# One branch a step, and another order of fetches, in a two-layer hybrid decoder trunk

## The chip, the core and the metric

The kernel runs as one program on one core of a Trainium2 chip. The metric is device time in microseconds, the median of several executions. The core has a matrix engine (TensorE, PE in the profile), VectorE (DVE), ScalarE (ACT), GpSimd (POOL) and SyncE (SP). Each takes its instructions in order. In this kernel SP issues nearly all DMAs, from memory into SBUF, and a DMA that must wait for its buffer holds up every DMA behind it.

## What is computed

256 tokens of width 1024 go through two layers, all in float32:

```python
h = x
for i in range(2):
    mix = forgetting_attention(h, ...) if i == 0 else ssd_mixer(h, ...)
    h = layer_norm(ALPHA * h + mix, ln_mix_g[i], ln_mix_b[i])
    ffn = swiglu(h, ...) if i == 0 else moe_swiglu(h, ...)
    h = layer_norm(ALPHA * h + ffn, ln_ffn_g[i], ln_ffn_b[i])
    h = h + (p[i] @ ple_w_proj[i]) * sigmoid(h @ ple_w_gate[i])
```

The second layer's feed-forward part has 8 experts, of which each token takes 2. An expert has a gate and an up matrix of 1024 x 3584 and a down matrix of 3584 x 1024:

```python
for e in range(8):
    y_e = (silu(x @ w_gate[e]) * (x @ w_up[e])) @ w_down[e]
    out = out + gates[..., e:e+1] * y_e
```

## The kernel before

All weights lie in memory as chunks of 128 x 2048 floats, 1024 KB each, in the order of their use. In SBUF there are 22 slots of one chunk each, `sf[0]` to `sf[21]` (`sr[i]` is the same memory under the type fp32r). Slots 20 and 21 are called TH and TL: up to the end of the mixer they hold the transposed tokens, split into a high and a low rounded part, and after it they take chunks like the others. Slots 0 and 1 hold token buffers in the expert stage, so 20 slots are left for chunks there. The constants `ck` (identity, triangles, iota) are a tile of their own.

**Layers up to the mixer** take each float32 product as three fp32r products (`mm3`, L213 to L215) of parts split by ScalarE (L153) and VectorE (L156). `fetch` issues a chunk's DMA on SP in four pieces (L139) into a slot of the ring `rq`; `load` adds the two splits, with a slot of the ring `wq` for the high part.

**The state-space mixer** works on 8 groups g. Its steps are written out by hand: `channels` (projections), `conv`, `mix_a` to `mix_y` (the scan inside a group), `decay(q)` (factors for two groups, `decs`), and `w_out(g, t)` (the output projection). Ahead of the experts, slots that are done with are refilled by `next_chunk(n)` (its DMA is at L1012), which fetches the next chunk of a fixed list `order` into slot n. These calls stand by hand among the mixer's steps: slots 13 and 14 in the group loop at g == 4, right behind `decay(3)`, which is the last to read them; slot 15, then TH and TL, then eleven more in the tail of the mixer, and the last four behind it.

**The experts** run as 56 steps (e, f), 7 per expert; a step takes 512 of the 3584 columns and has six chunks, four for gate and up and two for down. A step gathers no tokens itself: once per expert up to 96 tokens are gathered by a matmul with a one-hot matrix (`gather`). The first 64 of them go through `gate_up0` (L1386) and `down0` (L1422) with 64 columns of the array, the other 32 through `gate_up1` (L1393) and `down1` (L1429). The latter two stand each in an If on TensorE alone, `over(e)`, taken when expert e has more than 64 tokens; `L1591` and `L1580` are their lines. `turn_u` transposes the step's activations (L1412, L1413). The order of a step i on TensorE is: gate_up0(i), If gate_up1(i), down0(i-1), If down1(i-1), turn_u(i). Each `next_chunk` of a slot stands behind the part that reads it last. `y_out` copies the expert's sums out of PSUM (L1435, L1437) and `scatter` adds them to the tokens in the next step, with one float32 matmul per token half and column half (L1442).

In expert 7, f == 0, `pr`, the operand pT of the last projection (256 KB), is fetched (L1619) behind that step's `next_chunk` calls; it is multiplied at L1628 in f == 2 and 3. At f == 4 `beyond` (L1483) is an If on all engines around a long loop for experts with more than 96 tokens; with this data it is jumped over. Behind the experts come the last scatter, the LayerNorm and the gated embedding.

From the mixer on, the order on PE, ACT, DVE and SP is the order of the text (`manual_schedule`).

Of the kernel before, what the change touches and what calls it, by code (L numbers as in the profile page):

```python
# [17 lines left out]
P = 128  # L18
D = 1024
# [34 lines left out]
def trunk_kernel(ctx, tc, ws, xtok, xT, pT, lnp, cst, wsm, cw, gn, vec, out):  # L54
# [4 lines left out]
    nc.alloc_sbuf_tensor("slots", [P, N_SLOT * 2048 + 16], FT)  # L59
    base = (nc.sbuf_base - (N_SLOT * 2048 + 16) * 4 + 63) // 64 * 64  # L60
# [4 lines left out]
    sf = [place(f"sf{i}", 2048, FT, i) for i in range(N_SLOT)]  # L65
    sr = [place(f"sr{i}", 2048, FR, i) for i in range(N_SLOT)]
# [167 lines left out]
    ck = const.tile([P, K_END], FT, name="ck")  # L234
# [598 lines left out]
    with tc.tile_pool(name="ssd", bufs=1, reuse_waits="tile") as sd, tc.tile_pool(name="ssd2", bufs=2, reuse_waits="tile") as s2p:  # L833
        cwt = sd.tile([P, 32, 5], FT, name="cwt")
# [425 lines left out]
        next_chunk(TH)  # L1260
        next_chunk(TL)
# [13 lines left out]
        for n in rq[:-1] + wq[:-1] + [12, 16, 17]:  # L1275
            next_chunk(n)
# [25 lines left out]
    with tc.tile_pool(name="moe", bufs=1, reuse_waits="tile") as mo:  # L1302
        res = tokens(1)
        hx = sf[18].rearrange("p (t k q) -> p t k q", t=T, k=KT)
        strb = mo.tile([P, P], BF, name="strb")
        oneb = mo.tile([P, P], BF, name="oneb")
# [65 lines left out]
        def turn_s(s, name="sT", bufs=2):  # L1372
# [3 lines left out]
            sT = mo.tile([SLOTS, T, P], FT, name=name, bufs=bufs)  # L1376
            nc.vector.tensor_copy(sT, ps[0:SLOTS, 0:S].rearrange("p (t q) -> p t q", t=T))
            return sT
# [30 lines left out]
        def turn_u(u0, u1):  # L1409
# [3 lines left out]
            nc.tensor.transpose(ps[:, 2 * P:3 * P], u1, ident)  # L1413
            uT = mo.tile([P, 3 * P], FT, name="uT")
            nc.vector.tensor_copy(uT, ps[:, 0:3 * P])  # L1415
            return uT
# [8 lines left out]
        def down1(w, uT, y1, first, last):  # L1425
            for q in range(4):
                o = 2 * P + 32 * q
                for r in range(4):
                    nc.tensor.matmul(y1[32 * r:32 * r + 32, 0:S], uT[:, o:o + 32], w[q // 2][:, q % 2, r * S:(r + 1) * S],  # L1429
                                     start=first and q == 0, stop=last and q == 3)  # L1430

        def y_out():
            y = mo.tile([SLOTS, D], FT, name="y")
# [4 lines left out]
            return y  # L1438

        def put(sT, y, t, hf):  # L1440
            ps = pst()
            nc.tensor.matmul(ps, sT[:, t], y[:, HS[hf]], start=True, stop=True)  # L1442
            return ps
# [5 lines left out]
        def scatter(sT, y, gate):  # L1449
            for t in range(T):  # L1450
                for hf in range(2):
                    add(put(sT, y, t, hf), t, hf, gate)
# [19 lines left out]
        def beyond(most, n):  # L1472
# [10 lines left out]
            with tc.If(most > SLOTS):  # L1483
                xo = room()
# [5 lines left out]
                for first in range(SLOTS, S, SLOTS):  # L1490
                    nc.vector.memset(eid, 0.0)
                    with tc.For_i(0, E * N_EXP, N_EXP) as ie:
# [6 lines left out]
                        sTo = turn_s(so, "sTo", 1)  # L1499
                        gather(so, xo)  # L1500
                        for f in range(FC):
# [4 lines left out]
                            for h in range(2):  # L1506
# [4 lines left out]
                                for c in range(2):  # L1511
# [3 lines left out]
                                    uTo = mo.tile([P, SLOTS], FT, name="uTo")  # L1515
# [4 lines left out]
                        y = mo.tile([SLOTS, D], FT, name="y")  # L1520
                        for g in range(2):
                            nc.scalar.copy(y[:, HS[g]], yo[g][0:SLOTS])
                        scatter(sTo, y, [gte[:, t:t + 1] for t in range(T)])
# [42 lines left out]
        uTs, free = {}, []  # L1566
# [9 lines left out]
        def down(i):  # L1576
            e, f = steps[i]
            n, w = chunks([C_MOE + 6 * i + c for c in (4, 5)])
            down0(w, uTs[i], y0, f == 0, f == FC - 1)
            with over(e):  # L1580
                down1(w, uTs[i], y1, f == 0, f == FC - 1)
            del uTs[i]
            free.extend(n)

        xs_, sTs, ye = {0: x}, {0: sT}, {}
        for i, (e, f) in enumerate(steps):
# [3 lines left out]
            u0 = act0(p0)  # L1590
            with over(e):  # L1591
                gate_up1(w, xs_[e], p1)
            u1 = act1(p1)
            if (e, f) == (E - 1, 1):
                pjn = next(j for j in n if j < TH)
                n.remove(pjn)
            for j in n:
                next_chunk(j)
            if i > 0:
                down(i - 1)  # L1600
                for j in free:
                    next_chunk(j)
                free.clear()
            uTs[i] = turn_u(u0, u1)
            if f == 0 and e > 0:
                ye[e - 1] = y_out()
                nc.vector.memset(y1[:, 0:S], 0.0)
            if f == 1 and e > 0:
                scatter(sTs.pop(e - 1), ye.pop(e - 1), col(gt, e - 1))
# [6 lines left out]
            if (e, f) == (E - 1, 0):  # L1616
                most = nc.values_load(cni[0:1, 0:1], min_val=0, max_val=S)
                pr = mo.tile([P, 2, S], FT, name="u")
                nc.sync.dma_start(pr, pT[1])  # L1619
# [10 lines left out]
            if (e, f) == (E - 1, 4):  # L1630
                beyond(most, held[C_PLE1])
                next_chunk(held.pop(C_PLE1))
        lnw = sf[held.pop(-1)].rearrange("p (a d) -> p a d", a=2)
        down(len(steps) - 1)
        y = y_out()
# [14 lines left out]
        pp = [[put(sT, y, t, hf) for hf in range(2)] for t in range(T)]  # L1650
# [157 lines left out]
```

## Time and profile before

| | |
|---|---|
| median of 3 runs | 1509.65 us (1508.84 to 1510.35) |
| profiled execution | 1507.73 us |
| its span, first to last instruction | 1506.0 us |
| PE busy | 1439.5 us (96%) |
| DVE, ACT busy | 554.3 us (37%), 381.5 us (25%) |
| DMA | 458.62 MB, mean 305 GB/s |
| mean granted TensorE clock | 0.986 |

The span is what the trace covers, and the execution's own time lies 1.73 us above it. Times in the trace are counted from the span's start. In a timeline a row stands for a run of like instructions of one engine: its start, its length, engine, line, operation, out<-in, count, and in brackets how long the engine had stood idle and what ended that. In this kernel the attention, the dense feed-forward part and the mixer take the time up to about 600 us, the experts run from 619 to 1464 us, and the rest is the end.

### The profile page before, as it was taken

The numbers are of one execution on the slowest core, as the hardware profiler recorded it, in microseconds if no ns is written. First come the engines' busy times: TensorE is split into PE (matmuls) and PEld (weight loads), VectorE is DVE, ScalarE is ACT, GpSimd is POOL, SyncE is SP. The second block draws the span as 40 slices with busy tenths as digits, with TensorE's granted clock in tenths as the row PEclk, the third lists the DMA queues.
The fourth block names the chain that finished last, engine by engine and source line by source line (L and its number), as shares of the span: only waits on it lengthen the run. The fifth ranks groups of instructions, "written<-read, shape, count | busy, mean of one in ns | idle before, by whom it ended". The sixth has DMA issues, their size and how long they took to land. (4 is left out here: it accounts for less than half of the span.)

```text
span 1506.0 us, 23136 instructions
## 1 busy us (share of the span) xinstructions
PE 1439.5 (96%) x9451; PEld 885.0 (59%) x9451; DVE 554.3 (37%) x1117; ACT 381.5 (25%) x794; POOL 32.5 (2%) x41
## 2 busy tenths in 40 slices
PE   8999999999999899999999999999999999986887
PEld 6998999988999798534333333343334333332325
DVE  6667645557787667300111211101100202111017
ACT  6444544445675543200000000000000000000013
POOL 0000000000210001000000000000000000000000
PEclk9999999999999999999999999999999999999999
DMA  9423555556541745899899999999999999999960
GB/s 338 169 95 122 203 189 193 186 177 206 169 142 58 265 155 224 365 379 391 353 419 420 420 419 420 420 421 420 421 420 388 419 421 420 419 421 421 420 242 29
DMA packets 91705, 458.62 MB, mean 305 GB/s; under 512 B 10416, under 2 KB 10672, under 8 KB 44464
## 3 DMA queue, kind: packets, MB, share of 16 engines
q1 hardware_dynamic: 91280, 456.56, 76.7%
q8 instruction: 104, 1.70, 0.5%
q14 instruction: 33, 0.27, 0.1%
q10 hardware_dynamic: 288, 0.09, 0.0%
HBM read 455.56 MB, written 1.05 MB: 303 GB/s over the span
## 5 line engine op out<-in xcount | busy, mean ns | idle before, releaser
L1386 PE MATMUL ps<-sf,x 128*64 128x512 f32 x1792 | 400.6, 600 | 11.2 <-PEq L1483 6.0
L213 PE MATMUL ps<-sr,sr 128*128 128x256 f32 (+1 forms) x992 | 301.8, 304 | 7.7 <-ACT sr L153 6.1
L214 PE MATMUL ps<-sr,sr 128*128 128x256 f32 (+1 forms) x992 | 296.6, 299 | 1.2 <-DVE sr L156 1.2
L215 PE MATMUL ps<-sr,sr 128*128 128x256 f32 (+1 forms) x992 | 296.3, 299 | 0.2 <-DVE sr L352 0.2
L1386 PEld LDWEIGHTS ps<-sf,x 128*64 128x64 f32 x1792 | 124.7, 138 | 252.7 <-issue 235.3
L156 DVE TENSOR_TENSOR sr<-sf,sr 128x512 fp32r<-128x512 f32 (+1 forms) x306 | 225.3, 790 | 77.7 <-ACT sr L153 77.3
L1422 PE MATMUL ps<-sf,uT 128*64 128x512 f32 x896 | 204.9, 598 | 11.6 <-PEq L1591 9.8
L153 ACT CAST sr<-sf 128x512 fp32r<-128x512 f32 (+1 forms) x306 | 193.4, 698 | 70.5 <-DMA sf<-in_ws_dram 69.2
L213 PEld LDWEIGHTS ps<-sr,sr 128*128 128x128 f32 x992 | 191.4, 193 | 15.0 <-ACT sr L153 6.1
L214 PEld LDWEIGHTS ps<-sr,sr 128*128 128x128 f32 x992 | 191.6, 193 | 7.4 <-DVE sr L156 2.0
L215 PEld LDWEIGHTS ps<-sr,sr 128*128 128x128 f32 x992 | 191.2, 193 | 6.1 <-DVE sr L352 0.9
L1399 ACT ACTIVATE u<-ps 128x256 f32<-128x256 f32 x56 | 21.5, 383 | 605.2 <-PE ps L1386 605.2
L1400 DVE TENSOR_TENSOR u<-u,ps 128x256 f32<-128x256 f32 x56 | 23.6, 421 | 402.9 <-ACT u L1399 402.9
L1422 PEld LDWEIGHTS ps<-sf,uT 128*64 128x64 f32 x896 | 65.9, 136 | 140.5 <-issue 131.9
L1415 DVE COPY uT<-ps 128x384 f32<-128x384 f32 x56 | 31.2, 557 | 234.3 <-PE ps L1413 234.3
L1393 PE MATMUL ps<-sf,x 128*32 128x256 f32 x1344 | 76.9, 381 | 0.0
L1393 PEld LDWEIGHTS ps<-sf,x 128*32 128x32 f32 x1344 | 41.5, 110 | 42.3 <-issue 17.0
L1429 PE MATMUL ps<-sf,uT 128*32 128x256 f32 x672 | 40.6, 382 | 0.0
L1406 DVE TENSOR_TENSOR u<-u,ps 128x128 f32<-128x128 f32 x56 | 15.8, 282 | 64.7 <-ACT u L1405 64.7
L302 POOL TENSOR_TENSOR rp_r<-rp_a,mh 128x1 f32<-128x1 f32 (+1 forms) x16 | 12.4, 774 | 1245.9 <-DVE rp_a L301 1241.8
L885 DVE SCALAR_TENSOR_TENSOR xb<-ps,cwt,xb 128x255 f32<-128x255 f32 (+2 forms) x96 | 38.7, 471 | 0.6 <-ACT xb L876 0.6
L213 PE MATMUL ps<-sr,uh 128*128 128x512 f32 x96 | 37.6, 392 | 0.0
(273 smaller groups left out, 1137.2 us busy)
## 6 DMA issues: line engine op xcount, KB each, us to landing
sf<-in_ws_dram SPq DMA_DIRECT2D x364, 1024.0 KB, 19.6
sf<-in_ws_dram SPq DMA_DIRECT2D x252, 256.0 KB, 5.2
sf<-in_lnp_dram SPq DMA_DIRECT2D x4, 1024.0 KB, 5.1
sf<-in_xT_dram SPq DMA_DIRECT2D x4, 256.0 KB, 5.9
sf<-in_xtok_dram SPq DMA_DIRECT2D x1, 1024.0 KB, 8.5
ck<-in_cst_dram SPq DMA_DIRECT2D x1, 608.0 KB, 5.7
u<-in_pT_dram SPq DMA_DIRECT2D x2, 256.0 KB, 11.5
out_dram<-sf SPq DMA_DIRECT2D x1, 512.0 KB, 2.6
```

Of the source, the lines that this page charges most:

```text
L153: cp = nc.scalar.copy(sr[m][:, c], src)
L156: x = eng.tensor_sub(dst, src, sr[m][:, c].bitcast(FT))
L213: nc.tensor.matmul(ps, lh, rh, start=start, stop=False)
L214: nc.tensor.matmul(ps, lh, rl, start=False, stop=False)
L215: nc.tensor.matmul(ps, ll, rh, start=False, stop=stop_)
L885: nc.vector.scalar_tensor_tensor(r[:, i, k:S], ps[:, i, 0:S - k], cwt[:, ch[i], 3 - k:4 - k], r[:, i, k:S], op0=OP.mult, op1=OP.add)
L1386: nc.tensor.matmul(p0[64 * h:64 * h + 64], x[:, kk, 0:64], w[c][:, k, HS[h]], start=kk == 0, stop=kk == KT - 1)
L1393: nc.tensor.matmul(p1[32 * q:32 * q + 32, 0:S], x[:, kk, 64:SLOTS], w[c][:, k, q * S:(q + 1) * S], start=kk == 0, stop=kk == KT - 1)
L1400: nc.vector.tensor_mul(u, u, pv[:, :, 1])
L1415: nc.vector.tensor_copy(uT, ps[:, 0:3 * P])
L1422: nc.tensor.matmul(y0[64 * h:64 * h + 64], uT[:, o:o + 64], w[q // 2][:, q % 2, HS[h]], start=first and q == 0, stop=last and q == 3)
L1429: nc.tensor.matmul(y1[32 * r:32 * r + 32, 0:S], uT[:, o:o + 32], w[q // 2][:, q % 2, r * S:(r + 1) * S], start=first and q == 0, stop=last ...
```

## The change

Six edits:

1. Slots TH and TL move up in SBUF by a gap of 2248 floats; the constants `ck`, the convolution weights, and in the expert stage `strb`, `oneb`, `y` and `yl` are put into that gap.
2. `next_chunk(13)` and `next_chunk(14)` move from g == 4 to behind the group loop. TH and TL move to behind the first three slots of `rq`, and the other slots of the tail come in another order.
3. A step's order becomes gate_up0(i), transpose of the narrow activations (`turn_u1`), down0(i-1), transposes of the wide ones (`turn_u0`), and one If with gate_up1(i) and down1(i-1). Only where an expert ends (f == 0) does down1 stand in an If of its own. All `next_chunk` calls of a step stand behind that If.
4. The scatter of experts 0 to 6 takes y in two fp32r parts, yh and yl (`y_split`, `scatter2`). The last expert's stays.
5. `pr` goes into a slot taken from the ring in step (6, 1) and is fetched there; the slot comes back in step (7, 4). The slot of the projection's result is taken in (7, 0) and not in (7, 1).
6. `values_load` of the largest count stands ahead of step (7, 0)'s `next_chunk` calls.

```diff
+    GAP = 2248
+    nc.alloc_sbuf_tensor("slots", [P, N_SLOT * 2048 + GAP + 16], FT)
...
+    sf = [place(f"sf{i}", 2048, FT, i, GAP if i >= TH else 0) for i in range(N_SLOT)]
...
-    ck = const.tile([P, K_END], FT, name="ck")
+    ck = place("ck", K_END, FT, TH)
...
-            if g == 4:
-                decay(3)
-                next_chunk(13)
-                next_chunk(14)
+            if g == 4: decay(3)
             conv_act(g, 1)
         g = G - 1
+        next_chunk(13)
+        next_chunk(14)
         lnw = load_ln(2)
...
-        next_chunk(TH)
-        next_chunk(TL)
...
-        for n in rq[:-1] + wq[:-1] + [12, 16, 17]:
+        for n in rq[:3] + [TH, TL] + rq[3:4] + wq[:2] + [12, 16, 17] + rq[4:-1] + wq[2:-1]:
             next_chunk(n)
...
+        def scatter2(sT, yh, gate):
+            for t in range(T):
+                for hf in range(2):
+                    ps = pst()
+                    nc.tensor.matmul(ps, sT[:, t], yh[:, HS[hf]], start=True, stop=False)
+                    nc.tensor.matmul(ps, sT[:, t], yl[0:SLOTS, HS[hf]], start=False, stop=True)
+                    add(ps, t, hf, gate)
...
+        def down_0(i):
+            uT1 = turn_u1(u1)
+            n, w = chunks([C_MOE + 6 * i + c for c in (4, 5)])
+            f = steps[i][1]
+            down0(w, uTs.pop(i), y0, f == 0, f == FC - 1)
+            return lambda: down1(w, uT1, y1, f == 0, f == FC - 1), n
+
         for i, (e, f) in enumerate(steps):
             n, w = chunks([C_MOE + 6 * i + c for c in range(4)])
             p0 = pst()
             gate_up0(w, xs_[e], p0)
             u0 = act0(p0)
+            rest, free = down_0(i - 1) if i > 0 else (None, [])
+            if f == 0 and e > 0:
+                with over(e - 1):
+                    rest()
+                y_out()
+                nc.vector.memset(y1[:, 0:S], 0.0)
+            uTs[i] = turn_u0(u0)
             with over(e):
                 gate_up1(w, xs_[e], p1)
+                if f > 0:
+                    rest()
             u1 = act1(p1)
-            if (e, f) == (E - 1, 1):
+
+            if (e, f) == (E - 1, 0):
+                most = nc.values_load(cni[0:1, 0:1], min_val=0, max_val=S)
                 pjn = next(j for j in n if j < TH)
                 n.remove(pjn)
-            for j in n:
+            if (e, f) == (E - 2, 1):
+                prn = next(j for j in n if j < TH)
+                n.remove(prn)
+                pr = place("pr", 2 * S, FT, prn).rearrange("p (a s) -> p a s", a=2)
+                nc.sync.dma_start(pr, pT[1])
+            for j in n + free:
                 next_chunk(j)
-            if i > 0:
-                down(i - 1)
-                for j in free:
-                    next_chunk(j)
-                free.clear()
-            uTs[i] = turn_u(u0, u1)
...
             if f == 1 and e > 0:
-                scatter(sTs.pop(e - 1), ye.pop(e - 1), col(gt, e - 1))
+                scatter2(sTs.pop(e - 1), yh, col(gt, e - 1))
```

## Rows read from the trace of the kernel before

**Rows 1.** The page, busy time of each engine.

```profile
PE 1439.5 (96%) x9451; PEld 885.0 (59%) x9451; DVE 554.3 (37%) x1117; ACT 381.5 (25%) x794; POOL 32.5 (2%) x41
```

**Rows 2.** Stretches: length, busy time of each engine, granted clock, DMA share, GB/s.

```profile
516.00:523.00 7.00, 5.43 (x25) 5.46 (x26) 6.81 (x14) 4.81 (x11) 0.00 (x0) 0.52 1.06 393
627.00:740.00 113.00, 112.65 (x999) 46.49 (x991) 9.20 (x23) 5.19 (x15) 0.00 (x0) 1.00 0.90 366
740.00:1140.00 400.00, 393.71 (x2765) 155.70 (x2761) 55.42 (x128) 24.30 (x69) 0.00 (x0) 1.00 1.01 419
1347.00:1395.00 48.00, 28.54 (x113) 9.22 (x113) 7.87 (x16) 2.27 (x6) 0.00 (x0) 0.88 1.01 420
1395.00:1446.00 51.00, 43.56 (x164) 15.47 (x166) 2.97 (x8) 4.00 (x10) 0.00 (x0) 0.88 1.00 412
```

**Rows 3.** Timeline of one heavy step, expert 0; SP's refetches in it.

```profile
647.04 7.09 PE L1386 MATMUL ps<-sf,x 128*64 128x512 f32 x32
654.06 3.66 PE L1393 MATMUL ps<-sf,x 128*32 128x256 f32 x64
655.20 8.37 SPq L1012 DMA_DIRECT2D sf<-in_ws_dram  x6
657.65 3.65 PE L1422 MATMUL ps<-sf,uT 128*64 128x512 f32 x16
661.24 1.93 PE L1429 MATMUL ps<-sf,uT 128*32 128x256 f32 x32
663.10 0.44 PE L1412 MATMUL ps<-ck,u 128*128 128x128 f32 x2
...
663.58 7.09 PE L1386 MATMUL ps<-sf,x 128*64 128x512 f32 x32
```

**Rows 4.** Timeline of expert 7: TensorE, and ScalarE's last copy.

```profile
1352.47 7.07 PE L1386 MATMUL ps<-sf,x 128*64 128x512 f32 x24 [4.85 <-DMA sf<-in_ws_dram]
...
1395.39 6.14 PE L1628 MATMUL ps<-sf,u 128*128 128x512 f32 x8 [12.97 <-DMA u<-in_pT_dram]
1401.46 7.09 PE L1386 MATMUL ps<-sf,x 128*64 128x512 f32 x32
1408.86 3.65 PE L1422 MATMUL ps<-sf,uT 128*64 128x512 f32 x16 [0.31 <-PEq L1591]
1412.66 0.41 PE L1412 MATMUL ps<-ck,u 128*128 128x128 f32 x2
...
1434.25 8.87 PE L1386 MATMUL ps<-sf,x 128*64 128x512 f32 x32 [5.98 <-PEq L1483]
...
1463.65 1.19 ACT L1435 COPY y<-ps 64x512 f32<-64x512 f32 x2 [8.44 <-PEq L1580]
```

**Rows 5.** One line's instructions: the chunk fetches of next_chunk, L1012.

```profile
L1012 SPq DMA_DIRECT2D sf<-in_ws_dram x337: 327/328/1190, 499.0 to 1425.8; - x169
...
DMA to landing us min/median/max: 4.7/19.8/21.0
```

**Rows 6.** SP: a wait (total, times, longest us), and the timeline.

```profile
SPq L1012 <- PE ps L959: 36.3, 1, 36.3
...
499.00 0.81 SPq L1012 DMA_DIRECT2D sf<-in_ws_dram  x2
```

**Rows 7.** Timeline of TensorE in the mixer, groups 4 and 5.

```profile
513.32 0.72 PE L1118 MATMUL ps<-ck,y 128*128 128x128 f32 x4 [2.19 <-ACT sr L153]
515.24 0.30 PE L1041 MATMUL ps<-ck,xb 128*128 128x128 f32 x1 [1.20 <-DVE xs L1036]
...
517.57 0.55 PE L213 MATMUL ps<-sr,sr 128*128 128x256 f32 x1 [1.59 <-ACT yh L1125]
```

**Rows 8.** Timeline of SP: the first fetch into a slot given back.

```profile
627.00 0.33 SPq L1012 DMA_DIRECT2D sf<-in_ws_dram  x1
```

**Rows 9.** One line's instructions: compare-branches, ns min/median/max, of two Ifs.

```profile
L1591 PEldq COMPARE_BRANCH  x77: 70/179/447, 621.5 to 1450.2; - x77
...
L1483 PEldq COMPARE_BRANCH  x1: 6136/6136/6136, 1427.8 to 1427.8; - x1
```

More of the change, by code (lines that the diff above doesn't have):

```diff
@@ L56, in trunk_kernel @@
     N_SLOT, TH, TL = 22, 20, 21
-    nc.alloc_sbuf_tensor("slots", [P, N_SLOT * 2048 + 16], FT)
-    base = (nc.sbuf_base - (N_SLOT * 2048 + 16) * 4 + 63) // 64 * 64
+    GAP = 2248
+    nc.alloc_sbuf_tensor("slots", [P, N_SLOT * 2048 + GAP + 16], FT)
+    base = (nc.sbuf_base - (N_SLOT * 2048 + GAP + 16) * 4 + 63) // 64 * 64
     def place(name, n, dt, slot, first=0):
         return nc.alloc_sbuf_tensor_at(name, [P, n], dt, offset=base + 4 * (2048 * slot + first)).ap()
-    sf = [place(f"sf{i}", 2048, FT, i) for i in range(N_SLOT)]
-    sr = [place(f"sr{i}", 2048, FR, i) for i in range(N_SLOT)]
+    sf = [place(f"sf{i}", 2048, FT, i, GAP if i >= TH else 0) for i in range(N_SLOT)]
+    sr = [place(f"sr{i}", 2048, FR, i, GAP if i >= TH else 0) for i in range(N_SLOT)]
     pieces = {}
@@ L1303, in trunk_kernel @@
         res = tokens(1)
+        y, yl = (place(n, D, dt, TH, K_END) for n, dt in (("y", FT), ("yl", FR)))
         hx = sf[18].rearrange("p (t k q) -> p t k q", t=T, k=KT)
-        strb = mo.tile([P, P], BF, name="strb")
-        oneb = mo.tile([P, P], BF, name="oneb")
+        strb, oneb = (place(n, P, BF, TH, K_END + o) for n, o in (("strb", 0), ("oneb", P // 2)))
         nc.gpsimd.tensor_copy(strb, ck[:, K_STR:K_STR + P])
@@ L1375, in turn_s @@
                 nc.tensor.transpose(ps[0:SLOTS, TS[t]], s[:, t], ident)
-            sT = mo.tile([SLOTS, T, P], FT, name=name, bufs=bufs)
+            sT = room_s() if sT is None else sT
             nc.vector.tensor_copy(sT, ps[0:SLOTS, 0:S].rearrange("p (t q) -> p t q", t=T))
@@ L1437, in y_out, with y_split, put @@
                 nc.vector.tensor_copy(y[64:SLOTS, r * S:(r + 1) * S], y1[32 * r:32 * r + 32, 0:S])
-            return y
-        def put(sT, y, t, hf):
+        def y_split():
+            yh = mo.tile([SLOTS, D], FR, name="yh")
+            nc.scalar.copy(yh, y[0:SLOTS])
+            nc.vector.tensor_sub(yl[0:SLOTS], y[0:SLOTS], yh.bitcast(FT))
+            return yh
+        def put(sT, t, hf):
             ps = pst()
-            nc.tensor.matmul(ps, sT[:, t], y[:, HS[hf]], start=True, stop=True)
+            nc.tensor.matmul(ps, sT[:, t].bitcast(FT), y[0:SLOTS, HS[hf]], start=True, stop=True)
             return ps
@@ L1519, in beyond @@
                                                          start=f == 0 and q == 0, stop=f == FC - 1 and q == 3)
-                        y = mo.tile([SLOTS, D], FT, name="y")
                         for g in range(2):
-                            nc.scalar.copy(y[:, HS[g]], yo[g][0:SLOTS])
-                        scatter(sTo, y, [gte[:, t:t + 1] for t in range(T)])
+                            nc.scalar.copy(y[0:SLOTS, HS[g]], yo[g][0:SLOTS])
+                        scatter(sTo, [gte[:, t:t + 1] for t in range(T)])
             banks[:] = b5
@@ L1565, in trunk_kernel @@
         nc.vector.memset(y1[:, 0:S], 0.0)
-        uTs, free = {}, []
+        uTs = {}
         def over(e):
@@ L1574, in chunks @@
             return n, [sf[i].rearrange("p (k n) -> p k n", k=2) for i in n]
-        def down(i):
-            e, f = steps[i]
+        xs_, sTs = {0: x}, {0: sT}
+        def down_0(i):
+            uT1 = turn_u1(u1)
             n, w = chunks([C_MOE + 6 * i + c for c in (4, 5)])
[L1579 to L1585, printed above, removed]
+            f = steps[i][1]
+            down0(w, uTs.pop(i), y0, f == 0, f == FC - 1)
+            return lambda: down1(w, uT1, y1, f == 0, f == FC - 1), n
         for i, (e, f) in enumerate(steps):
@@ L1632, in trunk_kernel @@
                 next_chunk(held.pop(C_PLE1))
+                next_chunk(prn)
         lnw = sf[held.pop(-1)].rearrange("p (a d) -> p a d", a=2)
-        down(len(steps) - 1)
-        y = y_out()
+        rest, free = down_0(len(steps) - 1)
+        with over(E - 1):
+            rest()
+        y_out()
         for j in free:
@@ L1649, in trunk_kernel @@
         gate_w(0)
-        pp = [[put(sT, y, t, hf) for hf in range(2)] for t in range(T)]
+        pp = [[put(sT, t, hf) for hf in range(2)] for t in range(T)]
         st0 = new_stats()
```

39 lines of the change are left out of this document (20 added, 19 removed).

## The prediction

> **What bounds the kernel now.** The page comes first: TensorE is busy for 96% of the span, so time is won where TensorE stands still, or where it is made to do less [rows 1]. That share is an average over stages, so the next view is the table of stretches. In the expert stage the DMA engines deliver 366 GB/s while expert 0 runs (627 to 740 us), 419 over the next 400 us, 420 and 412 at the end [rows 2]. About 419 is what they can do here: one 1024 KB chunk in 2.50 us, the six chunks of a step in 15.0.
>
> Third, the steps themselves. A step whose expert has more than 64 tokens (heavy) takes TensorE 663.58 - 647.04 = 16.54 us [rows 3]. A light one takes 1408.86 - 1401.46 = 7.40 and 3.80 [rows 4], and 0.48 for its transposes [rows 3]: 11.68. So TensorE is slower than the fetches in heavy steps and faster in light ones. Which experts are heavy is seen by whether L1393 stands between L1386 and L1422: in 0, 3 and 4. In expert 0 all 20 slots in use are full, and a fetch starts when a slot is given back: that is where 366 GB/s come from. Over experts 1 to 6 TensorE lives on that stock. At 1347 it is used up, with a wait of 4.85 us for a chunk, the first long one in the stage [rows 4]. From there the end of the stream of chunks sets the time, if nothing else holds TensorE.
>
> Something else does. It waits 12.97 us for pT, which was issued behind eight 1 MB chunks, and 5.98 us at L1483; so it ends the stage late. The last expert chunk is issued at 1425.8 and lands at most 21.0 us later, at 1446.8 [rows 5], but the last sum is copied out at 1463.65 [rows 4]: 16.9 us of lag that no chunk asks for. After that comes the tail, which the chain of waits shows and the change leaves alone: 42.35 us to the end of the span.
>
> Ahead of the experts one place stands out. SP waits 36.3 us in next_chunk at L1012 for decay(3) and issues two chunks at 499.00 [rows 6]. The weight pieces of groups 5 and 6 stand behind them and come late, in a burst. TensorE stalls for 2.19 + 1.20 + 1.59 = 4.98 us [rows 7], and the 7 us after it run at a granted clock of 0.52, nearly all at the lower level, 1.2 GHz [rows 2].
>
> **The change part by part.** The sum is made against the profiled execution: a span of 1506.0 us in 1507.73 us. The median of the runs shown, 1509.65, is 1.92 above it.
>
> *Chunks for slots 13 and 14 after the group loop.* SP no longer waits for decay(3) with weights queued behind it. The stall of 4.98 goes. At half clock the 5.43 us of TensorE work in 516 to 523 would have taken 52% of that, so 2.6 more. What these two chunks are now queued ahead of is the load of LayerNorm 2 and the last three weights: 5.0 us of transfer, against weights that are used only behind both channel blocks of group 7. If the weights were late anyway, the gain is nothing; it is below nothing only if those 5.0 us made the last weights late, by 5.0 at most. More than 7.6 there is not. I take 7.6.
>
> *Order of the slots in the tail of the mixer.* A blocked slot no longer holds up free ones. But the 20 chunks are fetched before the first slot is given back: the first refetch starts at 627.00, set by TensorE in step 0 [rows 8]. Earlier arrivals make that queue idle longer, nothing else: 0. If the cover were gone (chunks still missing when step 0 wants a refetch) it would be worth the 4.7 us that the quickest fetch needs from issue to landing [rows 5].
>
> *One branch a step.* TensorE's order becomes gate/up of the first 64 slots (6.9), one transpose (0.2), the down projection of the step before (3.5), two transposes (0.3), then one If with the narrow gate/up (3.5) and the narrow down (1.8). Its work is the same. No row shows what the edges of an If cost; two of four go, while the transposes become two groups. Bounds: 0, and two median branches of 0.179, so 0.36 [rows 9]; I take 0.1 for a heavy step, since the second transpose group takes part of it back, and 0.2 for a light one. In light steps fetches cover it; in heavy ones I count 0.6 over expert 0.
>
> *Later release, which that order brings.* A heavy step gives its first gate slot back 655.20 - 647.04 = 8.16 us after its start [rows 3]. The narrow gate/up now stands behind the down projection and all transposes: 6.9 + 0.2 + 3.5 + 0.3 + 0.2 + its first quarter 0.9 and the same 0.25 to the issue = 12.2, so 4.1 later. In expert 0 every fetch waits for such a release, so the stream of chunks runs 4.1 - 0.6 = 3.5 later against TensorE's start; at the change to expert 1, where all six slots come back together after its transposes, about 0.6 more. Behind that the stream is full for 700 us and cannot catch up. I take +4.1; the bounds are 0 (releases don't hold the stream) and 8.2 (each release of the step shifts a whole narrow part more).
>
> *Scatter in two rounded parts.* It takes the place of four full matmuls of two records each. What eight fp32r records take lies between nothing and the 6.14 us of the eight full ones at L1628 [rows 4]. ScalarE and VectorE make the two parts in a step in which they are mostly idle. It happens between experts, where fetches cover it: 0, from -1 (one scatter inside expert 3 or 4) to +2.
>
> *The projection's operand fetched in expert 6.* The 12.97 us wait goes. Next late is the chunk itself: TensorE is then up to 15 us ahead of where it was, so it waits for chunks again, and the wait at L1483 (the far branch stays) falls into time in which it would wait for gate chunks. The end is then last chunk + second half of the down projection 1.8 + 0.5 for the skip and the start of the copy, so a lag of 2.3 in place of 16.9: 14.6 saved. Bounds: 11 (the far branch, and the lower clock behind it, still leave TensorE 4 us late) and 15.5. The two slots lent to this operand and to the result cost nothing while the queue, not a free slot, is the limit there.
>
> *Token buffers and constants moved in SBUF.* No row shows an address. Bounds: 0, and a loss if both moved slots took chunks as slowly as the worst stretch (366 against 419, on 2 of 20 slots over 700 us: 9 us). I take 0: slots at 20 different addresses feed a steady 419 now.
>
> Sum: -7.6 + 4.1 - 14.6 = -18.1. Span 1487.9, execution 1489.6, and by the 1.92 above it, a median of **1491.5 us**.
>
> **Rivals.**
> A. *The long skip.* In 35 light steps the one branch jumps over 128 + 64 = 192 weight loads and matmuls in place of 128 and then 64. L1483 shows what a jump too far costs: 6.14 us, against at most 0.45 for either short one [rows 9]. At that price a light step takes 11.4 + 5.7 = 17.1, is slower than the fetches, and 35 x 5.4 = 189 us come on; less the 17.8 of waits for chunk and operand and the 7.6 of the mixer, about 1673 us. It decides from 4 us a skip, where light steps become as slow as their six chunks; below it the fetches cover all. For it: the jump is half as long again. Against: 64 and 128 cost the same. 5%. The Trainium skill, "Runtime: NRT & Kernel Launch", section Instruction fetch mechanics, says that a taken branch whose target is outside the two pages of 256 instructions at hand waits until the target's page is fetched. By that rule, 192 instructions stay within reach; the trace agrees as far as 64 and 128 go, at 0.45 us or less, and L1483 is what a miss looks like.
> B. *The weights are late anyway* or another wait comes in the mixer: no 7.6. Then 1499. For it: ScalarE and VectorE split those weights and are half busy there. Against: groups 2 to 4 ran without a stall at the same rhythm. 12%.
> C. *TensorE stays late at the end*: L1483 at the low clock eats 4 us, or moved slots or releases cost 4 more: 1495 to 1500. 15%.
> D. *Releases don't hold the stream*, since slots are free by then: no 4.1. Then 1487. 10%.
> E. *The operand is late again*, or the skip and releases together eat the gains: within 0.2%. 3%.
>
> **How the numbers follow.** The forecast has 55%; its own range, from the bounds of release and tail, is 1487 to 1496. With B to D to either side 1485 to 1500 holds some 8 in 10. Anything within 0.2% (3 us) can't be told from no change here. Faster: the forecast, B, C, D = 0.92; same 0.03; slower: A = 0.05.
>
> **What would show it.** Mixer: no long wait of SP at L1012 before 500 us, no TensorE gap and no low clock near 516, and step 0 near 611 in place of 618.8 (8.16 ahead of 627.00). Release: the first gate slot 12 us after a heavy step's start, and less than 366 GB/s in expert 0. Tail: no wait for pT, waits for chunks in the last five steps, and the copy of the last sum 2 to 3 us after the last chunk. It is wrong if compare-branches in light steps take over 1 us, if that copy still lags by over 8, or if the stream is not full between expert 1 and the end.

## Result, and the profile after

| | median, us | range | ratio to the kernel before, 95% interval |
|---|---|---|---|
| kernel before | 1509.66 (4 runs) | 1508.84 to 1510.35 | |
| kernel after | 1491.24 (4 runs) | 1488.83 to 1492.31 | 0.9876 (0.9859 to 0.9893) |

The time lies 0.3 us from the forecast. The profiled execution took 1490.5 us with a span of 1488.7, against 1506.0 before: 17.3 less. Where they come from is another matter, and three moments show it. The first step of the experts starts 13.64 us earlier (605.22 against 618.86), the last expert chunk lands only 3.8 earlier, and the last sum is copied out 17.3 earlier. So 13.6 were won ahead of the experts, 9.8 of them were lost again in the stream of chunks, and 13.5 were won at the end. The forecast had 7.6, 4.1 and 14.6. The sum was right because two errors cancel, which is luck. The first step of the experts, before and after:

```profile
618.86 7.09 PE L1386 MATMUL ps<-sf,x 128*64 128x512 f32 x32
```

```profile
605.22 7.09 PE L1388 MATMUL ps<-sf,x 128*64 128x512 f32 x32
```

A single execution's start of the experts carries some us of its own: the granted clock between 560 and 610 us was 0.90 to 1.00 from one kernel's profiled execution to another's (1.00 before, 0.97 after). The medians of the runs stand beside it for that reason.

The edits moved the line numbers: mm3 is now L215 to L217, `next_chunk` L1014, `gate_up0` L1388, `gate_up1` L1395, the transposes L1414 and L1421, `down0` L1430, `down1` L1437, the copy of the sums L1442, `beyond` L1504, the If L1617.

The page, busy time of each engine (for [rows 1]):

```profile
PE 1432.5 (96%) x9451; PEld 878.3 (59%) x9451; DVE 566.1 (38%) x1180; ACT 392.3 (26%) x801; POOL 32.5 (2%) x41
```

TensorE has the same number of matmul records, in 7 us less of busy time.

Stretches of the kernel after (for [rows 2]); the columns are as there. The first is the place of the old stall, the second expert 0:

```profile
503.00:510.00 7.00, 7.00 (x62) 7.00 (x62) 5.15 (x12) 5.63 (x13) 0.00 (x0) 1.00 0.49 154
...
614.00:727.00 113.00, 113.00 (x1012) 47.42 (x1000) 9.22 (x29) 5.21 (x15) 0.00 (x0) 1.00 0.87 351
...
1120.00:1175.00 55.00, 54.70 (x431) 24.11 (x429) 10.30 (x25) 5.43 (x12) 0.00 (x0) 1.00 0.91 373
```

The stall in the mixer is gone: TensorE is busy for all of the 7 us, at the full clock, 2.4 GHz. In expert 0 the DMA engines deliver less than before, 351 GB/s against 366. The last row is a window that [rows 2] do not have: around the end of the heavy experts 3 and 4 the stream runs at 373 GB/s. The kernel before had 398 in the same window, where expert 4 ends 9 us later:

```profile
1120.00:1175.00 55.00, 54.69 (x435) 23.07 (x435) 6.95 (x18) 3.99 (x10) 0.00 (x0) 1.00 0.97 398
```

A heavy step of expert 0, TensorE and SP (for [rows 3]):

```profile
633.75 7.09 PE L1388 MATMUL ps<-sf,x 128*64 128x512 f32 x32
640.77 0.33 PE L1421 MATMUL ps<-ck,u 128*128 128x128 f32 x1
641.03 3.65 PE L1430 MATMUL ps<-sf,uT 128*64 128x512 f32 x16
644.62 0.44 PE L1414 MATMUL ps<-ck,u 128*128 128x128 f32 x2
644.98 3.66 PE L1395 MATMUL ps<-sf,x 128*32 128x256 f32 x64
...
646.11 4.64 SPq L1014 DMA_DIRECT2D sf<-in_ws_dram  x6
...
650.30 1.08 PE L1388 MATMUL ps<-sf,x 128*64 128x512 f32 x4
```

The step takes 650.30 - 633.75 = 16.55 us, as before. Its first gate slot comes back 646.11 - 633.75 = 12.36 us after its start; the forecast said 12.2.

Where two heavy experts end, at 1143 us: the one chunk issued there, and its time to landing.

```profile
L1014 SPq DMA_DIRECT2D sf<-in_ws_dram x1: 328/328/328, 1143.2 to 1143.2; - x1
...
DMA to landing us min/median/max: 4.9/4.9/4.9
```

4.9 us is what a chunk takes when nothing is ahead of it in the queue [rows 5]: the stream had run dry.

The tail: TensorE's waits for chunks (total, times, longest us), its timeline, ScalarE's last copy (for [rows 4]), and the last fetches of chunks, in this order. PEq stands for a wait that an instruction of TensorE's own queue ended, here the branch at that line.

```profile
PE ps L1388 <- DMA sf<-in_ws_dram: 14.7, 18, 6.2
PE ps L1430 <- DMA sf<-in_ws_dram: 7.6, 18, 0.6
```

```profile
1416.00 9.58 PE L1388 MATMUL ps<-sf,x 128*64 128x512 f32 x32 [6.66 <-PEq L1504]
...
1446.33 1.19 ACT L1442 COPY y<-ps 64x512 f32<-64x512 f32 x2 [4.69 <-PEq L1660]
```

```profile
L1014 SPq DMA_DIRECT2D sf<-in_ws_dram x7: 327/328/328, 1406.7 to 1421.6; - x7
...
DMA to landing us min/median/max: 19.8/21.1/21.1
```

The 12.97 us for pT no longer stand among TensorE's waits; it waits for chunks in their place. The last chunk is issued at 1421.6 and lands 21.1 later, at 1442.7. The sum is copied out 3.6 us behind that, where it was 17.1 (its own landing before is 1446.54). From the copy to the end of the span it is 42.37 us, before 42.35.

### The profile page after: what moved, and what is told of

Same layout as the page of the kernel before. It is cut to its first block, busy times and chain, and to the rows that moved or that the text cites. A ratio compares the mean times of both kernels' runs of the same rounds, so it can differ in the third digit from the quotient of the medians.

```text
span 1488.7 us, 23115 instructions
## 1 busy us (share of the span) xinstructions
PE 1432.5 (96%) x9451; PEld 878.3 (59%) x9451; DVE 566.1 (38%) x1180; ACT 392.3 (26%) x801; POOL 32.5 (2%) x41
## 5 line engine op out<-in xcount | busy, mean ns | idle before, releaser
L1388 PE MATMUL ps<-sf,x 128*64 128x512 f32 x1792 | 405.0, 601 | 25.8 <-DMA sf<-in_ws_dram 14.7
L215 PE MATMUL ps<-sr,sr 128*128 128x256 f32 (+1 forms) x992 | 299.1, 302 | 5.8 <-ACT sr L155 5.8
L217 PE MATMUL ps<-sr,sr 128*128 128x256 f32 (+1 forms) x992 | 293.8, 296 | 0.7 <-DVE sr L354 0.7
L1388 PEld LDWEIGHTS ps<-sf,x 128*64 128x64 f32 x1792 | 130.4, 138 | 268.6 <-issue 231.7
L1430 PE MATMUL ps<-sf,uT 128*64 128x512 f32 x896 | 206.6, 599 | 7.6 <-DMA sf<-in_ws_dram 7.6
L215 PEld LDWEIGHTS ps<-sr,sr 128*128 128x128 f32 x992 | 187.9, 189 | 13.3 <-ACT sr L155 5.8
L217 PEld LDWEIGHTS ps<-sr,sr 128*128 128x128 f32 x992 | 187.6, 189 | 7.3 <-DVE sr L354 1.4
L216 PEld LDWEIGHTS ps<-sr,sr 128*128 128x128 f32 x992 | 187.8, 189 | 6.4 <-DVE sr L158 0.4
L1430 PEld LDWEIGHTS ps<-sf,uT 128*64 128x64 f32 x896 | 58.7, 136 | 113.6 <-issue 88.4
L1407 ACT ACTIVATE u<-ps 128x128 f32<-128x128 f32 x56 | 15.6, 278 | 273.6 <-PE ps L1395 147.2
L1416 DVE COPY uT<-ps 128x256 f32<-128x256 f32 x56 | 23.8, 425 | 160.7 <-PE ps L1414 160.5
L1395 PE MATMUL ps<-sf,x 128*32 128x256 f32 x1344 | 76.9, 380 | 0.0
L1395 PEld LDWEIGHTS ps<-sf,x 128*32 128x32 f32 x1344 | 41.5, 110 | 28.8 <-issue 3.5
L1437 PE MATMUL ps<-sf,uT 128*32 128x256 f32 x672 | 40.2, 379 | 0.0
```

The costliest lines, as they stand in the source:

```text
L215: nc.tensor.matmul(ps, lh, rh, start=start, stop=False)
L216: nc.tensor.matmul(ps, lh, rl, start=False, stop=False)
L217: nc.tensor.matmul(ps, ll, rh, start=False, stop=stop_)
L1388: nc.tensor.matmul(p0[64 * h:64 * h + 64], x[:, kk, 0:64], w[c][:, k, HS[h]], start=kk == 0, stop=kk == KT - 1)
L1395: nc.tensor.matmul(p1[32 * q:32 * q + 32, 0:S], x[:, kk, 64:SLOTS], w[c][:, k, q * S:(q + 1) * S], start=kk == 0, stop=kk == KT - 1)
L1416: nc.vector.tensor_copy(uT, ps[:, 0:2 * P])
```

## Experiments

Each ratio is taken against the kernel before, timed on the same chip. Differences against the kernel after are taken between ratios, times 1509; by the two intervals together such a difference is uncertain by about 3.5 us.

### The addresses alone, and the change without them

The first is the kernel before with the buffers TH and TL 8992 bytes further on (and the constants in the gap); the second is the kernel after with the gap behind all slots.

```diff
 # a1: before, this alone
-    sf = [place(f"sf{i}", 2048, FT, i) for i in range(N_SLOT)]
+    sf = [place(f"sf{i}", 2048, FT, i, GAP if i >= TH else 0) for i in range(N_SLOT)]
...
 # a2: after, this undone
-    sf = [place(f"sf{i}", 2048, FT, i, GAP if i >= TH else 0) for i in range(N_SLOT)]
+    sf = [place(f"sf{i}", 2048, FT, i) for i in range(N_SLOT)]
...
-    ck = place("ck", K_END, FT, TH)
+    ck = place("ck", K_END, FT, N_SLOT)
...
```

> Kernel before with one part of the change alone: the two token buffers (and constants, cwt, strb, oneb, y) at their new addresses. Theory (addresses): the 128x256 matmuls of mm3, whose starts stand 120.9 ns apart before and 118.2 ns after between 50 and 300 us, get quicker by the address of their moving operand; step 0 of the experts starts 5 us earlier than before (about 613.6 in place of 618.9) and the time is 1504.5 us, spacing about 118 ns. Rival (the spacing comes from something else in the change, such as the order of loads): spacing 121 ns, no gain, 1509.7 us. My prediction had 0 for this part.

> Kernel after with the two token buffers back at their old addresses; the room for constants stands behind all slots, every other tile where it is in the kernel after. Theory (addresses): spacing of the 128x256 matmuls back to about 121 ns, step 0 about 5 us later (610.4), time 1496.4 us. Rival (spacing not from these addresses): 118 ns and 1491.2 us.

Measured: a1 1503.98 us, ratio 0.9968 (0.9954 to 0.9981); a2 1495.23 us, ratio 0.9904 (0.9888 to 0.9919). The edit gives 4.8 us alone, and 4.2 go when it is undone. The rows are the commonest matmul of mm3 between 50 and 500 us (busy us, mean ns of one), in the kernels before, after, a1 and a2, in this order:

```profile
L213 PE MATMUL ps<-sr,sr 128*128 128x256 f32 x707 | 203.1, 287 | 0.0
L214 PE MATMUL ps<-sr,sr 128*128 128x256 f32 x707 | 200.0, 283 | 0.0
```

```profile
L215 PE MATMUL ps<-sr,sr 128*128 128x256 f32 x720 | 204.5, 284 | 0.0
L216 PE MATMUL ps<-sr,sr 128*128 128x256 f32 x720 | 201.3, 280 | 0.0
```

```profile
L214 PE MATMUL ps<-sr,sr 128*128 128x256 f32 x720 | 204.6, 284 | 0.0
```

```profile
L215 PE MATMUL ps<-sr,sr 128*128 128x256 f32 x704 | 202.1, 287 | 0.0
```

With the new addresses one takes 284 and 280 ns, with the old ones 287 and 283; more of them fit into the same window. In the profiled execution of a1 the experts start 3.7 us earlier than before (615.2 against 618.9), at a granted clock of 0.91 in place of 1.00 in 560 to 610 us; in that of a2 they start 8.6 later than after (613.8 against 605.2), at 0.93 in place of 0.97. The theory holds, and the 0 of the prediction was wrong.

### What in the address counts

In a partition the slots begin at a multiple of 64 bytes and each takes 8192, so TH begins at a multiple of 64 before; after, it lies 8992 bytes further on, which is 140 x 64 + 32. Both kernels are a2 with the two buffers moved by a little; the constants and `y`, which lie behind all slots there, move by the same k:

```diff
 # c2: k = 64 floats, 256 bytes; c3: k = 8 floats, 32 bytes
-    sf = [place(f"sf{i}", 2048, FT, i) for i in range(N_SLOT)]
+    sf = [place(f"sf{i}", 2048, FT, i, k if i >= TH else 0) for i in range(N_SLOT)]
...
```

> Kernel a2 (token buffers at their old addresses, 1495.2 us) with the two buffers 256 bytes further on, a multiple of 64 as before. Theory 1 (what counts is that the new address lies 32 bytes beside a multiple of 64): mean of a 128x256 matmul of mm3 stays at 283 to 287 ns in 50 to 500 us, 1495 us. Theory 2 (what counts is the place relative to the weight slots, which before lie at a distance that is a multiple of 8192 bytes): 280 to 284 ns, 1491 us. Theory 3 (the region of some 9 KB further on counts): 283 to 287 ns.

> Kernel a2 with the two token buffers 32 bytes further on. Theory 1 (32 bytes beside a multiple of 64): 280 to 284 ns for a 128x256 matmul of mm3 in 50 to 500 us, 1491 us. Theory 2 (place relative to the weight slots): 280 to 284 ns too, if 32 bytes are enough, else 283 to 287. Theory 3 (the region): 283 to 287 ns, 1495 us.

Measured: c2 1498.82 us, ratio 0.9936 (0.9917 to 0.9954); c3 1490.74 us, ratio 0.9882 (0.9866 to 0.9898). The same row in c2, then in c3:

```profile
L215 PE MATMUL ps<-sr,sr 128*128 128x256 f32 x709 | 203.6, 287 | 0.0
```

```profile
L215 PE MATMUL ps<-sr,sr 128*128 128x256 f32 x719 | 204.1, 284 | 0.0
```

32 bytes give all of the gain and 256 bytes none (by its ratio c2 is even slower than a2, but their profiled spans, 1496.6 and 1496.2 us, are the same). So theory 1 holds here: these matmuls are quicker when the token buffers that they read begin 32 bytes beside a multiple of 64. Some of them have the tokens as the moving operand, others as the stationary one, and the row does not part them. The region (theory 3) is out. That only a distance of 32 bytes from the weight slots helps, and 256 does not, says the same thing in other words, since all weight slots begin at a multiple of 64. Other offsets were not tried, and why it is so, no run shows. Not every matmul gains: those of 128x512 that have the tokens as their stationary operand took 395 to 402 ns after and 389 to 395 before (at 341 to 351 us before, 338 to 348 after). By the times the addresses are worth 4 to 8 us: 4.8 in a1, 4.2 in a2, and 8.1 between c2 and c3.

### The two chunks back in the group loop

```diff
-            if g == 4: decay(3)
+            if g == 4:
+                decay(3)
+                next_chunk(13)
+                next_chunk(14)
...
-        next_chunk(13)
-        next_chunk(14)
```

> Kernel after with the two chunks of slots 13 and 14 back in the group loop behind decay(3). Theory: SP waits some 36 us there again, TensorE stalls near 510 to 517 and step 0 of the experts starts 8.4 us later (613.6 in place of 605.2); all of the later stream moves with it: 1499.6 us. By my predicted term it would be 7.6 later: 1498.8. Rival B (the weights are late in any case, and all of the 13.6 us come from faster matmuls): 1491.2 us.

Measured: 1500.57 us, ratio 0.9945 (0.993 to 0.996), 10.4 us above the kernel after (9.3 between the medians). Its waits of SP (total, times, longest), and TensorE's timeline:

```profile
SPq L1014 <- PE ps L961: 35.9, 1, 35.9
```

```profile
509.34 0.72 PE L1120 MATMUL ps<-ck,y 128*128 128x128 f32 x4 [2.29 <-ACT sr L155]
511.26 0.39 PE L1043 MATMUL ps<-ck,xb 128*128 128x128 f32 x1 [1.20 <-DVE xs L1038]
...
513.60 0.56 PE L215 MATMUL ps<-sr,sr 128*128 128x256 f32 x1 [1.09 <-DVE xb L887]
```

The wait of SP and the three stalls of [rows 6, 7] are back, 2.29 + 1.20 + 1.09 = 4.6 us. In this execution the experts start 8.6 us later than in the one after, and the last expert chunk lands 8.8 later. The part of the prediction, 7.6, was right in kind and one or two us small. Rival B is out.

### The slots of the mixer's tail in their old order

```diff
-        for n in rq[:3] + [TH, TL] + rq[3:4] + wq[:2] + [12, 16, 17] + rq[4:-1] + wq[2:-1]:
+        for n in rq[:-1] + wq[:-1] + [12, 16, 17]:
...
         load()
+        next_chunk(TH)
+        next_chunk(TL)
```

> Kernel after with the old order of slots in the tail of the mixer (TH and TL first, then all of rq, wq, 12, 16, 17). My prediction: 0, since the first refetch is set by TensorE in step 0 and not by when the 20 chunks land: 1491.2 us. Rival: the order brings the first chunks of step 0 late, TensorE waits for one of them, and the experts start later by up to the 4.7 us that a fetch needs: up to 1496 us.

Measured: 1491.35 us, ratio 0.9887 (0.9869 to 0.9905). No difference can be told: 0, as forecast. The trace shows why: the last of the 20 chunks lands at 613.4, 10 us later than in the kernel after (603.2), but the first refetch starts 9.5 us after step 0 in both.

### The old order inside a step

```diff
             gate_up0(w, xs_[e], p0)
             u0 = act0(p0)
-            rest, free = down_0(i - 1) if i > 0 else (None, [])
...
-            uTs[i] = turn_u0(u0)
             with over(e):
                 gate_up1(w, xs_[e], p1)
-                if f > 0:
-                    rest()
             u1 = act1(p1)
...
-            for j in n + free:
+            for j in n:
                 next_chunk(j)
+            if i > 0:
+                rest, free = down_0(i - 1)
+                with over(steps[i - 1][0]):
+                    rest()
+                for j in free:
+                    next_chunk(j)
+            uTs[i] = turn_u0(u0), turn_u1(u1)
```

> Kernel after with the old order inside a step: gate/up of 64, If with the narrow gate/up, release of the gate slots, down projection of the step before, If with its narrow part, release of the down slots, both transposes; two branches a heavy or light step. All else as after. Theory (the release sets the stream): a heavy step gives its first slot back 8.2 us after its start again, in place of 12.4; the stream of chunks gets back the 6.4 us lost in expert 0 and, if the 4.2 us lost between 1140 and 1175 us have the same cause, these too; nothing behind holds TensorE, so the time falls by 6 to 10 us, to 1481 to 1485. By my predicted term alone, 4.1 less: 1487.1. Rival (releases do not hold the stream): 1491 to 1492, the second branch costing up to 0.1 a step.

Measured: 1480.65 us, ratio 0.9808 (0.9793 to 0.9822), 10.3 us *below* the kernel after. A heavy step of it, its SP row, and two of its stretches:

```profile
635.86 7.09 PE L1388 MATMUL ps<-sf,x 128*64 128x512 f32 x32
642.88 3.66 PE L1395 MATMUL ps<-sf,x 128*32 128x256 f32 x64
...
644.01 2.92 SPq L1014 DMA_DIRECT2D sf<-in_ws_dram  x4
...
652.40 1.08 PE L1388 MATMUL ps<-sf,x 128*64 128x512 f32 x4
```

```profile
616.00:729.00 113.00, 112.65 (x995) 46.42 (x987) 9.69 (x30) 5.21 (x15) 0.00 (x0) 1.00 0.90 367
1120.00:1175.00 55.00, 54.08 (x366) 22.70 (x359) 10.72 (x25) 5.03 (x12) 0.00 (x0) 1.00 1.00 414
```

The slot comes back 644.01 - 635.86 = 8.15 us after the start, 4.2 sooner, and the step is no longer: 652.40 - 635.86 = 16.54 with two Ifs, 16.55 with one. Expert 0 gets 367 GB/s in place of 351, the end of expert 4 gets 414 in place of 373. Its fetches between 1120 and 1170 us took at least 10.8 us to land, so the queue was never empty. Below them stands its last fetch of a chunk:

```profile
DMA to landing us min/median/max: 10.8/15.9/20.0
```

```profile
L1014 SPq DMA_DIRECT2D sf<-in_ws_dram x1: 328/328/328, 1415.3 to 1415.3; - x1
...
DMA to landing us min/median/max: 19.8/19.8/19.8
```

Counted from the start of step 0 (607.7 here, 605.2 after), the landings of this kernel run ahead of those of the kernel after by 4.4 us through expert 0 (chunk 56: 725.3 against 727.3), by 6.7 behind the change to expert 1 (chunk 68: 755.6 against 759.9), and by 10.0 behind expert 4 (the last: 1435.2 against 1442.7). So the release costs 4.4 + 2.3 + 3.3, where the prediction had 3.5 (4.1 less 0.6 for the branch), 0.6 and 0. From the start of step 0 to the last landing it is 827.5 us, as in the kernel before (827.7); in the kernel after it is 837.5. Rival D is out. The start itself differs by 2.4 between the two executions, since the granted clock before it does; kernel after, then this one, in 560 to 610 us:

```profile
560.00:610.00 50.00, 49.57 (x274) 38.13 (x274) 31.42 (x82) 18.48 (x38) 3.71 (x7) 0.97 0.79 316
```

```profile
560.00:610.00 50.00, 49.81 (x260) 39.78 (x260) 30.88 (x79) 15.68 (x37) 3.70 (x7) 0.90 0.78 316
```

### One If, ahead of the wide down projection

If the release is the cost, the one branch can be kept: its body moves ahead of `down0` and not behind it.

```diff
-            rest, free = down_0(i - 1) if i > 0 else (None, [])
...
-            uTs[i] = turn_u0(u0)
+            wide, rest, free = down_0(i - 1) if i > 0 else (None, None, [])
             with over(e):
                 gate_up1(w, xs_[e], p1)
                 if f > 0:
                     rest()
             u1 = act1(p1)
+            if i > 0:
+                wide()
...
+            uTs[i] = turn_u0(u0)
```

> Kernel after, with its one If a step (the narrow gate/up and the narrow down projection of the step before) placed ahead of the wide down projection instead of behind it: the gate slots come back 8.4 us after a heavy step's start, as in the old order, and there is one branch a step. Theory (only the moment of release counts): the same time as the old step order with its two branches, 1480.7 us. Rival (one branch less is worth 0.1 us in each of 18 heavy steps, as my prediction had it): 1479. Rival (releases are not it, and the two branches of the old order were the gain): 1491 us.

Measured: 1478.69 us, ratio 0.9794 (0.9781 to 0.9806). Its release in a heavy step:

```profile
632.65 7.09 PE L1388 MATMUL ps<-sf,x 128*64 128x512 f32 x32
...
641.06 8.21 SPq L1014 DMA_DIRECT2D sf<-in_ws_dram  x6
```

8.4 us after the step's start, as expected. This is the fastest version measured, some 12 us below the kernel after. Against the old order with two Ifs the intervals overlap, and from step 0 to the last landing the two take 827.9 and 827.5 us, so what the second branch costs stays below what this can tell; that the two branches were the gain is out.

### Gate slots back one by one

The old order, with the narrow part of each chunk right behind its wide part.

```diff
-            gate_up0(w, xs_[e], p0)
+            for c in range(4):
+                gate_up0(w, xs_[e], p0, (c,))
+                with over(e):
+                    gate_up1(w, xs_[e], p1, (c,))
             u0 = act0(p0)
-            with over(e):
-                gate_up1(w, xs_[e], p1)
```

> The old-order kernel (1480.7 us) with the gate/up cut by chunk: for each of the four chunks the wide part, then an If with the narrow part, so five Ifs a step. A heavy step gives its first gate slot back about 2.9 us after its start in place of 8.2, and the fourth at 10.8 as before. Theory (release): the stream is then held by the down slots only, about 2.5 to 2.8 us sooner in expert 0 and as much at the end of expert 4: 1475 to 1478 us. Rival (three more Ifs in each step cost 0.2 to 0.45 each, on the path in 18 heavy steps): 1485 to 1500 us.

Measured: 1516.8 us, ratio 1.0048 (1.0035 to 1.0061). The rival wins, and by more than it said. A heavy step, and its first fetch:

```profile
637.84 1.94 PE L1388 MATMUL ps<-sf,x 128*64 128x512 f32 x8
639.71 1.07 PE L1395 MATMUL ps<-sf,x 128*32 128x256 f32 x16
640.71 1.94 PE L1388 MATMUL ps<-sf,x 128*64 128x512 f32 x8
...
640.84 3.20 SPq L1014 DMA_DIRECT2D sf<-in_ws_dram  x2
...
655.24 1.08 PE L1388 MATMUL ps<-sf,x 128*64 128x512 f32 x4
```

The slot comes back after 3.0 us, and early in expert 0 the stream is 4 us ahead of the old order (chunk 24 lands at 628.3 against 632.3). But the step takes 17.40 us: a pair takes 640.71 - 637.84 = 2.87, against a quarter of 7.02 + 3.59, 2.65. Four times 0.22 is the 0.87 that the step is longer. Light steps, which skip the narrow parts, went from 11.5 to 12.6 us by the three Ifs more. In heavy steps the Ifs and the more frequent change between 64 and 32 columns were not told apart. TensorE then hardly waits for chunks any more (1.1 us in all, after the old order 15.3): it is the bound, and the stream follows it. That an earlier release brings the next chunks earlier is confirmed; that it was cheap to get this way was wrong.

### The operand fetched late again

```diff
                 pr = place("pr", 2 * S, FT, prn).rearrange("p (a s) -> p a s", a=2)
-                nc.sync.dma_start(pr, pT[1])
...
+            if (e, f) == (E - 1, 0):
+                nc.sync.dma_start(pr, pT[1])
```

> Kernel after with pT fetched two steps later again, at the end of step (7,0), into the same slot. Theory: it is issued behind a backlog of chunks, lands 40 to 45 us after the step, and TensorE waits about 13 us for it; nothing behind has slack, so the lag between the last chunk and the copy of the last sum goes from 3.3 to about 16 us: 1504 us. By my predicted term 14.6: 1505.8. Rival (TensorE waits for chunks there anyway and the operand is hidden among them): 1491 us.

The fetch moves from step (6, 1) to step (7, 0), which is six steps later and not two.

Measured: 1500.2 us, ratio 0.9937 (0.9925 to 0.9949), 9.2 us above the kernel after. SP, TensorE and ScalarE:

```profile
1371.37 0.33 SPq L1644 DMA_DIRECT2D pr<-in_pT_dram  x1
...
1389.49 5.18 PE L1653 MATMUL ps<-sf,pr 128*128 128x512 f32 x8 [8.33 <-DMA pr<-in_pT_dram]
...
1458.27 1.19 ACT L1442 COPY y<-ps 64x512 f32<-64x512 f32 x2 [4.69 <-PEq L1661]
```

TensorE waits 8.3 us, and the sum is copied out 12.7 us behind the last chunk (landed at 1445.5), against 3.6. So 9.1 of the lag are the operand, in the kernel as it is after. The wait is shorter than the 12.97 before; the other 4.4 of the lag that went come with the rest of the change and were not taken apart. No run undoes edit 6, or the slots of edit 5 by themselves.

### No far branch

```diff
             if (e, f) == (E - 1, 4):
-                beyond(most, held[C_PLE1])
                 next_chunk(held.pop(C_PLE1))
```

> Kernel after without the block for experts with more than 96 tokens (it is not entered with these inputs, and its branch is what stalls TensorE for 6.7 us in step (7,5)); left out is that block, so a larger expert would not be computed. Theory: the lag between last chunk and copy of the last sum, 3.6 us after, falls to the 2.1 that the chunk alone asks for, and TensorE waits for chunks instead: 1489.7 us. Rival (the 6.7 us and the low clock behind them are on the path): 1482 to 1485 us. My prediction: 1491 (the stall falls into waits for chunks).

Measured: 1487.84 us, ratio 0.9859 (0.9842 to 0.9876), 2.6 us below the kernel after, within the uncertainty; the lag in the trace says more. ScalarE's copy:

```profile
1444.57 1.19 ACT L1442 COPY y<-ps 64x512 f32<-64x512 f32 x2 [4.39 <-PEq L1659]
```

The last chunk landed at 1442.42, so the lag is 2.15 us in place of 3.6: that is the 2.3 which the forecast took for a tail that only the chunk holds. The branch and the low clock behind it ([6.66 <-PEq L1504], then a gate/up of 9.5 us in place of 7.0, at a granted clock of 0.73) are hidden but for 1.4 us. Rival C is true to that extent.

### The old scatter

```diff
-            if f == 0 and e > 0:
-                yh = y_split()
             if f == 1 and e > 0:
-                scatter2(sTs.pop(e - 1), yh, col(gt, e - 1))
+                scatter(sTs.pop(e - 1), col(gt, e - 1))
```

> Kernel after with each scatter as four full float32 matmuls again in place of eight of the rounded parts (6.1 us in place of 2.0 on TensorE, seven times). My prediction: 0 (from -1 to +2), fetches cover it: 1491.2. Theory now: two of the seven fall into the heavy experts 3 and 4, at whose end the stream ran dry for 3.7 us after; 8.2 us more of TensorE work in them delay the releases at 1140 to 1175 us by as much, and the stream with them: 1497 to 1499 us.

Measured: 1493.1 us, ratio 0.9888 (0.9874 to 0.9902), 1.8 us above the kernel after with intervals that overlap. Its scatter in expert 1:

```profile
745.77 3.67 PE L1455 MATMUL ps<-y,sT 96*128 96x512 f32 x8
```

With it that step took 15.1 us in place of 13.5: the rounded form saves 1.6 us, not the 4.1 that I had taken. The 6.1 came from [rows 4], where the eight records stand behind a wait of 12.97 us and ran at a granted clock of 0.59 (1395.4 to 1401.4 us); at the full clock they take 3.67. Against the kernel after the chunks land 0.7 us later up to 1130 us, and 3.8 later behind expert 4: two scatters of 1.6 each, in the two heavy experts. So the mechanism is as the theory says, its size 3.1 in place of 8.2. The prediction had 0, and a gain of 1 at most; by the landings it gained 3.1, which the times alone do not tell from 0.

## Why the prediction came out right

- **What bounds the kernel** was read rightly for expert 0, for the mixer and for the last waits of TensorE in expert 7; each edit that moves one of these moved the time. That experts 3 and 4 hold the stream too, and what the matmuls ahead of the experts take, was left out.
- **Its signs.** Step 0 began at 605 and not near 611, the last copy came 3.6 us behind the last chunk and not 2 to 3, and one of its three signs of being wrong came true: at 1143 us the stream was not full.
- **Mixer, -7.6.** The mechanism is shown; 8.6 us at the start of the experts, 9 to 10 in the time. "More than 7.6 there is not" was wrong by that much.
- **Slot order, 0.** Right.
- **One branch, 0.6 in heavy steps.** Not there: 16.55 against 16.54 us. In light ones it was hidden, as forecast. Rival A is out: the branches of the If, in ns min/median/max, are what they were in [rows 9], though they now skip 192 instructions.

```profile
L1617 PEldq COMPARE_BRANCH  x77: 70/180/428, 613.2 to 1437.9; - x77
```

- **Later release, +4.1.** This is the step that failed, though its beginning held. The release at 12.2 us (12.36 measured) was right, and so were the 4.1 us in expert 0 (4.4), but not the 0.6 taken off them for the branch. "About 0.6 more" at the change to expert 1 measured 2.3, and "Behind that the stream is full for 700 us and cannot catch up" hid a second loss: experts 3 and 4 are heavy for 14 steps running, TensorE falls behind, every slot is full again, and the late release costs 3.3 us once more. [rows 2] leave 1140 to 1347 us out. In the kernel before, the fetches issued between 1140 and 1170 landed after as little as 6.7 us, 2 us more than from an empty queue, and a release 4 us later uses that up:

```profile
DMA to landing us min/median/max: 6.7/10.6/13.4
```

  The term is 10.0, not 4.1.
- **Addresses, 0.** Wrong: -4 to -8 us. The argument was about DMA into the slots; nothing was asked about who reads the buffers, which is most of the matmuls up to the experts. This error has the other sign and about the size of the one above.
- **Scatter, 0.** -3.1 by the landings and -1.8 by time, from two scatters that stand in heavy steps; "it happens between experts" did not hold for experts 3 and 4.
- **Tail, -14.6.** The lag went from 17.1 to 3.6 us, 13.5: of what was missing, 1.4 are the far branch. Of the 13.5, 9.1 are the operand in the kernel as it is.

Put together from the two profiled executions: -13.6 + 9.8 - 13.5 = -17.3. A forecast of -18.1 against a measured -18.4 is thus no proof of its terms: the terms of the mixer and the tail were sound in kind, and that the sum came so near was luck.

## What to carry to other kernels

In a loop that is fed through a fixed set of buffers, the time from a step's start to its first release counts beside the work: order the readers so that a buffer comes free early, and count what a late release costs once for every stretch in which the consumer is the slower side, not once for the whole loop. A table over a long stretch hides such places; look for the few tens of microseconds in which a fetch lands as quickly as from an empty queue. And when a sum comes out right, undo its terms one by one, those set to 0 too.

## What the runs showed of the hardware

- A 128 x 256 matmul of fp32r parts took 280 to 284 ns with the token buffer that it reads 32 bytes beside a multiple of 64 in the partition, and 283 to 287 ns with it at a multiple of 64 (means of some 700 each; two places of either kind). Over the layers up to the experts the times say 4 to 8 us.
- Changing between matmuls of 64 and of 32 columns nine times in a step in place of three, with three Ifs more around them, cost 0.87 us a heavy step, without an idle gap in the rows. Three skipped Ifs more cost a light step 1.1 us.
- A jump over a long block cost TensorE 6.7 us under a full DMA queue, and its next gate/up ran 9.5 us in place of 7.0, at a granted clock of 0.73; all but 1.4 us of it were hidden behind chunks that were not there yet.
